# A row mean on one core: rows in parts of 16, 96 and 16, two stores behind the last load, and the last scaling on GpSimd

## The chip, the cores and the metric

One core of a Trainium2 chip. The metric is the device time of one execution in microseconds, median of several runs. "Span" is the profiled part of an execution, some 1.5 us shorter. Executions of one kernel mostly agree within 0.3%.

## The reference

```python
batch, seq, dim = 32, 512, 1024            # x: float32, 67.1 MB
def reference(x, divisor):                 # divisor = 1024.0
    return (np.sum(x, axis=-1) / divisor).astype(np.float32)
```

16384 rows of 4 KiB are read once, and one float is written for each.

## The kernel before

Each of the 128 partitions handles 128 rows: 112 of the main part and 16 of the last part, each contiguous in memory (the pitch from one partition to the next is 448 KiB in the main part and 64 KiB in the last). All loads are on one queue, into three bulk tiles in turn, then into small tiles of their own. VectorE (DVE) sums; ScalarE (ACT) takes some rows late in the kernel. The last two rows of a partition are cut to shorten the work after the last byte.

```python
    L = 16
    M = J - L                                    # 112
    x_main = bass.AP(tensor=x.tensor, offset=0, ap=[[M * D, P], [D, M], [1, D]])
    x_last = bass.AP(tensor=x.tensor, offset=P * M * D, ap=[[L * D, P], [D, L], [1, D]])
    # ... o_main and o_last alike
    main = [(2, 0)] + [(14, 0)] * 6 + [(14, 4), (12, 5)]      # (rows, of them on ACT)
    last = [(8, 4), (4, 2), (2, 1)]
    # ...
    res = one.tile([P, M], F32, name="res")
    fin = one.tile([P, L], F32, name="fin")
    q = one.tile([P, L], F32, name="q")
    r = one.tile([P, L], F32, name="r")
    nc.gpsimd.memset(r, 0.0)
    # ... loads and sums of main (into res) and of last (into q)
    c = 768
    row = one.tile([P, D], F32, name="row")
    load(row, x_last[:, j, :])
    act_sum(r[:, j : j + 1], row[:, c:], by=scale)
    nc.vector.reduce_sum(out=q[:, j : j + 1], in_=row[:, :c], axis=AX)

    a, b = 448, 704
    # ... pa, pb, pc: the last row's columns [:a], [a:b], [b:], each with its own load
    nc.gpsimd.tensor_scalar_mul(out=res, in0=res, scalar1=scale)
    tc.keep_in_program_order(nc.sync.dma_start(out=o_main, in_=res))

    act_sum(pc[:, D - b : D - b + 1], pa)
    nc.vector.reduce_sum(out=pc[:, D - b + 1 :], in_=pb, axis=AX)
    nc.vector.scalar_tensor_tensor(
        out=fin[:, : L - 1], in0=q[:, : L - 1], scalar=scale, in1=r[:, : L - 1], op0=MULT, op1=ADD
    )
    scaled = one.tile([P, D - b + 2], F32, name="scaled")
    nc.vector.tensor_scalar(
        out=scaled, in0=pc, scalar1=scale, scalar2=0.0, op0=MULT, op1=ADD, accum_out=fin[:, L - 1 :]
    )
    tc.keep_in_program_order(nc.sync.dma_start(out=o_last, in_=fin))
```

## Time and profile before

| | before |
|---|---|
| time, median of 4 runs | 161.5 us (161.36 to 161.53) |
| span of the profiled run | 159.8 us |
| DVE, ACT, GpSimd busy | 121.1, 19.6, 0.8 us |
| moved | 67.18 MB, 420 GB/s |
| end of the last DVE instruction | 158.28 us |

The prediction shows the lines and reads them. What to look for: the DMA rows are full from start to end, so the time is that of the bytes plus a tail; and in the tail DVE is the last to be ready. In the lines of the profile, L176 is line 176 of the kernel, SPq the queue that issues the DMAs, DVEq or ACTq the queue in front of that engine, and "issue" time in which the profile shows nothing waited for; the merged chain follows what ended last back through what released it. Below I also use the trace's landing records: each load signals from all sixteen DMA engines, and its landing is the last of the sixteen. They are not a printed view, so they stand in tables.

### The profile page before, as it was taken

Reading aid. Unit: us, or ns where it says so; the run is one execution under the profiler, and the core shown is the slowest. Engines: PE = TensorE matmul, PEld = TensorE weight load, DVE = VectorE, ACT = ScalarE, POOL = GpSimd, SP = SyncE. Lnnn points to the kernel's source line nnn. Section 1 sums busy time; section 2 is a strip of 40 time slices with the busy share of each in tenths; the row PEclk is TensorE's granted clock in tenths of the full one; section 3 lists DMA queues with packets and bytes.
Section 4 is the critical chain, followed back from the end, with each engine's and each line's share of the span. In section 5 each row is a group of like instructions: output and inputs, shape, how many; then the busy total and the mean of one; then the engine's idle time right before and its main releaser. Section 6 shows DMA issues by size and latency. Waiting matters only on the chain.

```text
span 159.8 us, 139 instructions
## 1 busy us (share of the span) xinstructions
DVE 121.1 (76%) x17; ACT 19.6 (12%) x37; POOL 0.8 (0%) x6
## 2 busy tenths in 40 slices
DVE  0500059995999599978999599959995996494985
ACT  3000000000000000000000000000001900480973
POOL 0000000000000000000000000000000000001000
DMA  7999999978999999978999999978999999899993
GB/s 250 472 459 459 459 459 459 459 330 359 459 459 459 459 459 459 459 316 373 459 459 459 459 459 459 416 345 388 459 459 427 394 480 505 353 435 390 408 400 132
DMA packets 2592, 67.18 MB, mean 420 GB/s; under 512 B 544, under 2 KB 928, under 8 KB 1056
## 3 DMA queue, kind: packets, MB, share of 16 engines
q1 hardware_dynamic: 2592, 67.18, 98.0%
HBM read 67.11 MB, written 0.07 MB: 420 GB/s over the span
## 4 chain that ended last, share of the span: by engine, by line
DMA 76%; DVE 22%; SPq 1%; issue 0%; DVEq 0%
DMA t<-in_x_dram 56%; DMA row<-in_x_dram 21%; DVE res L153 20%; SPq L142 1%; DVE q L176 1%; DVE scaled L198 0%; DVE pc L193 0%; DVE fin L194 0%; DVEq L198 0%; DVEq L232 0%
## 5 line engine op out<-in xcount | busy, mean ns | idle before, releaser
L153 DVE TENSOR_REDUCE res<-t 128x14 f32<-128x14336 f32 (+3 forms) x9 | 111.2, 12360 | 34.3 <-DMA t<-in_x_dram 34.3
L147 ACT ACTIVATE junk<-t 128x1024 f32<-128x1024 f32 x16 | 16.2, 1013 | 135.9 <-DMA t<-in_x_dram 135.9
L153 DVE TENSOR_REDUCE q<-t 128x4 f32<-128x4096 f32 (+2 forms) x3 | 7.9, 2642 | 2.7 <-DMA t<-in_x_dram 2.5
L147 ACT ACTIVATION_READ_ACCUMULATOR junk<-t 128x1 f32 x16 | 3.0, 187 | 0.0
L147 ACT ACT_TABLE_LOAD x1 | 1.3, 1283 | 1.7 <-PEq L218 1.7
L189 POOL TENSOR_SCALAR res<-res 128x112 f32<-128x112 f32 x1 | 0.5, 494 | 143.8 <-DVE res L153 143.8
L176 DVE TENSOR_REDUCE q<-row 128x1 f32<-128x768 f32 x1 | 1.0, 953 | 0.0
L198 DVE TENSOR_SCALAR_CACHE_REDUCE scaled<-pc 128x322 f32<-128x322 f32 x1 | 0.5, 490 | 0.1
L147 ACT ACTIVATE junk<-pa 128x448 f32<-128x448 f32 x1 | 0.5, 548 | 0.0
L193 DVE TENSOR_REDUCE pc<-pb 128x1 f32<-128x256 f32 x1 | 0.4, 414 | 0.0
L147 ACT ACTIVATE junk<-row 128x256 f32<-128x256 f32 x1 | 0.4, 388 | 0.1
L194 DVE SCALAR_TENSOR_TENSOR fin<-q,r 128x15 f32<-128x15 f32 x1 | 0.2, 176 | 0.0
L147 ACT ACTIVATION_READ_ACCUMULATOR junk<-pa 128x1 f32 x1 | 0.2, 186 | 0.0
L147 ACT ACTIVATION_READ_ACCUMULATOR junk<-row 128x1 f32 x1 | 0.2, 185 | 0.0
L139 POOL MEMSET r<- 128x16 f32 x1 | 0.1, 112 | 1.3 <-POOLq L218 1.3
L218 POOL MEMSET const-bfloat16-1.0<- 128x1 bf16 x1 | 0.1, 103 | 0.0
L218 POOL MEMSET const-uint8-127<- 128x1 uint8 x1 | 0.1, 102 | 0.0
L218 POOL MEMSET const-float32-0.0<- 128x1 f32 x1 | 0.1, 99 | 0.2 <-issue 0.2
L218 POOL MEMSET const-float32-1.0<- 128x1 f32 x1 | 0.1, 99 | 0.0
L198 DVE DVE_READ_ACCUMULATOR scaled<-pc 128x1 f32 x1 | 0.1, 83 | 0.0
## 6 DMA issues: line engine op xcount, KB each, us to landing
t<-in_x_dram SPq DMA_DIRECT2D x7, 7168.0 KB, 35.7
t<-in_x_dram SPq DMA_DIRECT2D x1, 6144.0 KB, 33.3
t<-in_x_dram SPq DMA_DIRECT2D x1, 4096.0 KB, 26.1
t<-in_x_dram SPq DMA_DIRECT2D x2, 1024.0 KB, 18.6
t<-in_x_dram SPq DMA_DIRECT2D x1, 2048.0 KB, 30.5
row<-in_x_dram SPq DMA_DIRECT2D x1, 512.0 KB, 33.2
pa<-in_x_dram SPq DMA_DIRECT2D x1, 224.0 KB, 33.3
pc<-in_x_dram SPq DMA_DIRECT2D x1, 160.0 KB, 33.1
```

What stands on the lines that cost most here:

```text
L139: nc.gpsimd.memset(r, 0.0)
L142: tc.keep_in_program_order(nc.sync.dma_start(out=dst, in_=src))
L147: nc.scalar.activation(junk[:, :n], src, COPY, scale=by, accum_out=dst)
L153: nc.vector.reduce_sum(out=dst[:, :d], in_=t[:, :d, :], axis=AX)
L176: nc.vector.reduce_sum(out=q[:, j : j + 1], in_=row[:, :c], axis=AX)
L189: nc.gpsimd.tensor_scalar_mul(out=res, in0=res, scalar1=scale)
L193: nc.vector.reduce_sum(out=pc[:, D - b + 1 :], in_=pb, axis=AX)
L194: nc.vector.scalar_tensor_tensor(out=fin[:, : L - 1], in0=q[:, : L - 1], scalar=scale, in1=r[:, : L - 1], op0=MULT, op1=ADD)
L198: nc.vector.tensor_scalar(out=scaled, in0=pc, scalar1=scale, scalar2=0.0, op0=MULT, op1=ADD, accum_out=fin[:, L - 1 :])
L218: nc = _bacc.Bacc("TRN2", target_bir_lowering=False, num_devices=1)
```

## The change

The intent: take the scaling of the first 15 results of the last part off DVE, which ends last, and give it to GpSimd; recut the last two rows to suit; scale the results of the main part in two tiles as they come, and store both behind the last load. The reads change with it: parts of 16, 96 and 16 rows per partition.

```diff
-    main = [(2, 0)] + [(14, 0)] * 6 + [(14, 4), (12, 5)]
+    parts = [[(2, 0), (14, 0)], [(14, 0)] * 5 + [(14, 4), (12, 5)]]
     last = [(8, 4), (4, 2), (2, 1)]
 ...
+    def rows_of(first, n):
+        return bass.AP(tensor=x.tensor, offset=first * P * D, ap=[[n * D, P], [D, n], [1, D]])
 ...
-    res = one.tile([P, M], F32, name="res")
+    res = [one.tile([P, n], F32, name=f"res{k}") for k, n in enumerate(sizes)]
-    r = one.tile([P, L], F32, name="r")
-    nc.gpsimd.memset(r, 0.0)
+    r = one.tile([P, 1], F32, name="r")
 ...
+        nc.gpsimd.tensor_scalar_mul(out=res[k], in0=res[k], scalar1=scale)     # after each part
 ...
-    c = 768
+    c = 688
-    act_sum(r[:, j : j + 1], row[:, c:], by=scale)
+    act_sum(r, row[:, c:], by=scale)
-    a, b = 448, 704
+    a, b = 480, 672
 ...
-    nc.gpsimd.tensor_scalar_mul(out=res, in0=res, scalar1=scale)
-    tc.keep_in_program_order(nc.sync.dma_start(out=o_main, in_=res))
+    for k, n in enumerate(sizes):
+        tc.keep_in_program_order(nc.sync.dma_start(out=means_of(sum(sizes[:k]), n), in_=res[k]))
 ...
-    nc.vector.scalar_tensor_tensor(
-        out=fin[:, : L - 1], in0=q[:, : L - 1], scalar=scale, in1=r[:, : L - 1], op0=MULT, op1=ADD
+    nc.gpsimd.tensor_scalar_mul(out=fin[:, :j], in0=q[:, :j], scalar1=scale)
+    nc.gpsimd.tensor_scalar(
+        out=fin[:, j : j + 1], in0=q[:, j : j + 1], scalar1=scale, scalar2=r, op0=MULT, op1=ADD
     )
```

More of the change, by code (lines that the diff above doesn't have):

```diff
@@ L117, with means_of @@
     assert J * P == N
-    L = 16
-    M = J - L
-    x_main = bass.AP(tensor=x.tensor, offset=0, ap=[[M * D, P], [D, M], [1, D]])
-    x_last = bass.AP(tensor=x.tensor, offset=P * M * D, ap=[[L * D, P], [D, L], [1, D]])
-    o_main = bass.AP(tensor=out.tensor, offset=0, ap=[[M, P], [1, M]])
-    o_last = bass.AP(tensor=out.tensor, offset=P * M, ap=[[L, P], [1, L]])
-    main = [(2, 0)] + [(14, 0)] * 6 + [(14, 4), (12, 5)]
-    last = [(8, 4), (4, 2), (2, 1)]
-    assert sum(n for n, _ in main) == M and sum(n for n, _ in last) == L - 2
+    parts = [[(2, 0), (14, 0)], [(14, 0)] * 5 + [(14, 4), (12, 5)]]
+    last = [(8, 4), (4, 2), (2, 1)]
+    L = sum(n for n, _ in last) + 2
+    sizes = [sum(n for n, _ in p) for p in parts]
+    assert sum(sizes) + L == J
+    def rows_of(first, n):
+        return bass.AP(tensor=x.tensor, offset=first * P * D, ap=[[n * D, P], [D, n], [1, D]])
+    def means_of(first, n):
+        return bass.AP(tensor=out.tensor, offset=first * P, ap=[[n, P], [1, n]])
+    x_last = rows_of(sum(sizes), L)
+    o_last = means_of(sum(sizes), L)
     bulk = ctx.enter_context(tc.tile_pool(name="bulk", bufs=3))
@@ L153, in sums @@
         nc.vector.reduce_sum(out=dst[:, :d], in_=t[:, :d, :], axis=AX)
-    j = 0
-    for rows, on_act in main:
-        t = bulk.tile([P, 14, D], F32, name="t")
-        load(t[:, :rows, :], x_main[:, j : j + rows, :])
-        sums(res[:, j : j + rows], t, rows, on_act)
-        j += rows
+    for k, part in enumerate(parts):
+        x_part = rows_of(sum(sizes[:k]), sizes[k])
+        j = 0
+        for rows, on_act in part:
+            t = bulk.tile([P, 14, D], F32, name="t")
+            load(t[:, :rows, :], x_part[:, j : j + rows, :])
+            sums(res[k][:, j : j + rows], t, rows, on_act)
+            j += rows
+        nc.gpsimd.tensor_scalar_mul(out=res[k], in0=res[k], scalar1=scale)
     j = 0
```

## The prediction

> **What bounds the kernel now.** I read the page's chain first, because it says what kind of thing the time is, then the rows in slices, then the merged chain, the timeline of the last microseconds and the waits of the queue that issues the DMAs.
>
> ```profile
> DMA 76%; DVE 22%; SPq 1%; issue 0%; DVEq 0%
> ...
> DMA  7999999978999999978999999978999999899993
> GB/s 250 472 459 459 459 459 459 459 330 359 459 459 459 459 459 459 459 316 373 459 459 459 459 459 459 416 345 388 459 459 427 394 480 505 353 435 390 408 400 132
> ```
>
> Bytes bound it. The DMA row is at 7 to 9 from the first slice to the last but one; 67.18 MB in 159.8 us is 420 GB/s. The 22% of DVE in the chain is misleading: two of the six long reductions (15.1 us each) are in it because a bulk load is issued only when a buffer comes free, but the DMA row stays full beside them. The landings say so more sharply: the loads of 14 rows land at 4.80, 21.74, 38.69, 55.62 and so on, 16.94 us apart each time (the trace's landing records), which is 7.34 MB / 16.94 us = 433 GB/s without a gap. (The dips to 316 to 373 are an artefact of booking long packets into slices: the landings show no gap there.) So in the body only bytes per microsecond count, and what is not bytes is the tail after the last loads.
>
> The tail in order of time, from the merged chain:
>
> ```profile
> 122.91 33.25 DMA row<-in_x_dram
> 156.16 0.02 issue
> 156.18 0.96 DVE q L176
> 157.14 0.03 issue
> 157.17 0.18 DVE fin L194
> 157.34 0.34 DVE pc L193
> 157.68 0.04 DVEq L198
> 157.72 0.07 issue
> 157.79 0.49 DVE scaled L198
> 158.28 0.01 DVEq L232
> ```
>
> From the landing of the last whole row (156.16) to the end of DVE (158.28) the chain is DVE's alone, 2.12 us. The other inputs of the last instruction, from the timeline of the tail and the issues with their time to landing:
>
> ```profile
> 156.72 0.55 ACT L147 ACTIVATE junk<-pa 128x448 f32<-128x448 f32 x1
> ...
> 157.20 0.19 ACT L147 ACTIVATION_READ_ACCUMULATOR junk<-pa 128x1 f32 x1
> ...
> 158.31 0.34 SPq L201 DMA_DIRECT2D out_dram<-fin  x1
> ```
>
> ```profile
> pa<-in_x_dram SPq DMA_DIRECT2D x1, 224.0 KB, 33.3
> pc<-in_x_dram SPq DMA_DIRECT2D x1, 160.0 KB, 33.1
> pb<-in_x_dram SPq DMA_DIRECT2D x1, 128.0 KB, 33.1
> out_dram<-res SPq DMA_DIRECT2D x1, 56.0 KB, 11.5
> out_dram<-fin SPq DMA_DIRECT2D x1, 8.0 KB, 1.4
> ```
>
> pa was issued at 123.39, pb at 123.87, pc at 124.39, the store of res at 146.17, so they landed at 156.7, 157.0, 157.5 and 157.7. ACT was done at 157.39. DVE itself, done with pb at 157.68, was the last thing that the final instruction waited for: 0.18 us later than the data.
>
> ```profile
> SPq L232 <- DMA out_dram<-res: 0.6, 1, 0.6
> ...
> SPq L201 <- DVE scaled L198: 0.5, 1, 0.5
> ```
>
> The store of fin also waits for the first store, since the drain in front of it waits for every other DMA. That came at 157.7; then 0.5 us were waited for DVE. So the first store has about 0.5 us of slack, no more.
>
> **What the Trainium skill says.** (1) "DMA: Bandwidth & Descriptors", section Queues, rings and completion order: each DMA engine takes descriptors of a ring in order. The trace agrees: the res store issued at 146.17 landed at 157.7, just behind pc (157.5), though its data was ready. (2) The same page, section Latency and other measured facts, warns of row pitches in HBM at large powers of two: copies at 512 KiB ran at 207 GB/s per direction against 214 for a padded pitch, at 2 MiB 164. The change alters the pitch, from 448 KiB (112 rows of 4 KiB) to 64 and 384 KiB. The trace of before has 64 KiB too, in its last part: the packets of 32768 bytes there took 1216 ns, 26.9 bytes per ns; a 14-row packet, 57344 bytes in 2.118 us, is 27.1. No difference. 384 KiB is not tried in it. (3) "SBUF — State Buffer", section Who interferes with whom: GpSimd shares ports with DVE, but a tensor_reduce on trn2 never contends, nor does the tensor_scalar form that writes an accumulator; a DVE instruction with two SBUF inputs does. All that DVE still does beside GpSimd in the new tail is of the harmless kinds. The trace of before doesn't show an overlap that could test it: its one GpSimd scaling (145.65) ran while DVE was idle. (4) "Perfetto Trace Analysis", GPSIMD Engine Instruction, calls the reported length of a GpSimd instruction unreliable; so I take GpSimd's 494 ns as rough.
>
> **The change, part by part.**
>
> *Body.* The same bytes in loads of the same sizes and in the same order; the order of instructions on DVE and ACT is the same save one removed on DVE. Pitch aside, nothing changes: 0 us. The memset of r at 1.73 us goes; it was beside the first load: 0. The scaling of the first 16 results moves to some 37 us, beside the loads: 0.
>
> *Stores of res.* One store of 128 packets of 448 bytes becomes two, of 64 and of 384 bytes. The first can be issued after the wait at about 138, the second after 147.6; both are still behind pc in every ring, issued by 124.8. Per engine 8 packets each: the records show 448-byte packets starting 21 ns apart, so 8 x 21 = 0.17 us; for 384 bytes about 18.5 ns and for 64 bytes about 8 ns (estimates from these and from fin's packets), 8 x 26.5 = 0.21 us, plus one semaphore packet of 9 ns. So they land at about 157.76 in place of 157.71. Slack of 0.5 us becomes some 0.25 (the next paragraph moves the other side). Not on the path, but near.
>
> *DVE in the tail.* The instruction of 176 ns (L194) goes: with its gaps it held the chain from 157.14 to 157.26, where pb's reduction began beside its end, so 0.12 us. The row's reduction goes from 768 to 688 columns: 768 took 953 ns, 256 took 414, so 1.05 ns a column, 80 x 1.05 = 0.08 us. Thus row 156.18 to 157.05. pb's reduction is of 192 in place of 256, 414 - 67 = 347 ns; it can start when pb is there, about 157.0, at 157.04 at most: done at 157.39. Before it was 157.68, so DVE is free 0.29 us earlier.
>
> *What the last instruction waits for then.* ACT: 336 columns of row in place of 256. ACT's 448 took 548 ns and 256 took 388, so 0.83 ns a column; the row takes 0.455 us, its read begins at 156.57. The next can start 0.09 later, as the others do (start to start 1.04 us, read begun after 0.97), 156.66; but pa, 32 columns larger, lands at about 156.74 (16 KB at 433 GB/s is 0.04 us). 156.76 + 0.575 = 157.33, the read of the accumulator to 157.45. And pc lands at 157.5 still: the bytes up to its end are the same. So of DVE 157.39, ACT 157.45, pc 157.50, pc is the last. With 0.02 to 0.1 us of start the last instruction begins at about 157.56, not 157.79. It has 354 columns, not 322: 32 x 1.05 = 0.03 us more, 0.52. Its end: 158.08, not 158.28. Saved on the path: 0.23 - 0.03 = 0.20 us.
>
> *GpSimd.* Its second instruction of the tail needs the row's sum (157.05). GpSimd started 0.09 us after DVE's end at 145.56; at the full 494 ns of the 112-column form it would be done at 157.05 + 0.09 + 0.49 = 157.63, with one column likely by 157.3. Before 158.08 in either case. The first (14 columns) needs 156.16, 0.9 us earlier. Beside: 0.
>
> *The end.* Store of fin: same 8 KB, 1.4 us from issue. Sum: 159.8 - 0.2 = 159.6 us of span, 161.5 - 0.2 = 161.3 us of time. I choose to subtract from the median of 161.5, although the runs lie between 161.36 and 161.5; the saving is of the size of that spread.
>
> **The rivals.** (a) *The stores take DVE's place.* If the two small stores land 0.4 us later than I say, at 158.2 or so, the drain in front of the last store is what ends last and the gain is nil, or a loss of up to 0.2: 161.4 to 161.7. For it: both stores are behind the last load, their packets are small, and the drain passes several semaphores after the late one. Against it: 8 packets per engine cost nanoseconds each in the trace of before, and fin's 64-byte packets are 11 ns long. (b) *GpSimd ends last.* Needs a tail instruction of over 0.9 us, or two of 0.9 us from 156.2; against it 494 ns for 112 columns. It would give 161.5 to 161.8. (c) *The pitch of 384 KiB slows the body.* 96 of 128 rows are read so; 1% of rate there would be 1.2 us (0.75 of 156), and 2.8% (3.2 us) a whole verdict. For it only the page's row for 512 KiB; against it that this row lost 3% only and that in this trace engines, not HBM, set a constant rate (16.94 us each time, and the same at 64 KiB). It would make 162 to 165. (d) *The gain is hidden.* If pc or ACT comes a little later than I have it, the saving is 0.1: 161.4.
>
> **Range and chances.** The middle is 161.3. (d) and the spread of the runs, 0.14 us in three, widen it by 0.2 upward and downward, (a) and (b) some more upward, and a different state of the chip some both ways: 160.9 to 161.7. A gain of 2% would be 3.2 us, more than the whole tail from 156.16: almost excluded, 0.01. A loss of 2% needs (c) at its worst or an oversight: 0.02. Within 2%: 0.97.
>
> **What would show it right or wrong.** Right: landings of the 14-row loads still 16.94 us apart; in the chain, no fin on DVE, the row's reduction about 0.87 us, the last DVE instruction starting at about 157.5 to 157.6 and 0.52 us long, waiting for pc or ACT rather than for DVE; the queue still waiting for DVE before the store of fin, issued at about 158.1; 2736 packets (128 more of data, 16 more of semaphores). Wrong by (a): the wait of the queue for out_dram as the last one, and the store issued later than DVE's end by over 0.1. By (b): GpSimd the last before the store. By (c): landings over 17 us apart in the middle part. What would make the number wrong with the steps right is a shift of all loads by a few tenths, which the first landing (4.80) would show.

## The result, and the profile after

161.87 us (161.55 to 162.17, 4 runs) against 161.5: ratio 1.0024, 95% interval 1.0004 to 1.0045. That is within 2%, but outside the predicted range and on the wrong side: 0.2 us less was expected, 0.37 us more came. The runs also spread more: 161.42 to 162.17 over the 14 runs that the changed kernel had in all.

The page of the changed kernel counts the packets forecast:

```profile
DMA packets 2736, 67.18 MB, mean 419 GB/s; under 512 B 688, under 2 KB 1072, under 8 KB 1200
```

The end of its merged chain:

```profile
123.65 33.83 DMA pa<-in_x_dram
157.47 0.02 issue
157.50 0.57 ACT junk L151
158.07 0.13 ACTq L240
158.20 0.03 issue
158.23 0.05 DVEq L206
158.28 0.08 issue
158.35 0.52 DVE scaled L206
158.88 0.01 DVEq L240
```

DVE's own work no longer sets the end. The chain now runs from the landing of pa through ACT to the last DVE instruction. And everything is later: pa landed at 157.47, not at the 156.7 of before. The timeline of the tail has DVE's and GpSimd's part of it, and the queue's waits the store:

```profile
156.79 0.87 DVE L183 TENSOR_REDUCE q<-row 128x1 f32<-128x688 f32 x1
...
157.76 0.35 DVE L200 TENSOR_REDUCE pc<-pb 128x1 f32<-128x192 f32 x1
157.76 0.27 POOL L202 TENSOR_SCALAR fin<-q,r 128x1 f32<-128x1 f32 x1 [0.71 <-DVE q L183]
...
158.91 0.33 SPq L209 DMA_DIRECT2D out_dram<-fin  x1
```

```profile
SPq L240 <- DMA out_dram<-res: 1.0, 1, 1.0
...
SPq L209 <- DVE scaled L206: 0.3, 1, 0.3
```

GpSimd (POOL) is done at 158.03, long before DVE. The queue still waits for DVE last, 0.3 us after the stores of res. So neither GpSimd nor the stores hold the end. Where the time went, by the landing records and the lines above (us):

| stretch | before | after | difference | predicted difference |
|---|---|---|---|---|
| start to the first landing | 4.80 | 4.86 | +0.06 | 0 |
| first landing to that of the 12-row load | 133.12 | 133.52 | +0.40 | 0 |
| 12-row load to 8-row load | 9.71 | 9.70 | -0.01 | 0 |
| 8-row load to row | 8.53 | 8.69 | +0.16 | 0 |
| row's landing to the end of DVE | 2.12 | 2.11 | -0.01 | -0.20 |
| end of DVE to the end of the span | 1.48 | 1.47 | -0.01 | 0 |

The differences add up to 0.59 us, that of the spans (159.76 and 160.35). Three things are to be explained: 0.40 us lost in the body, 0.16 us lost in the last loads, and a tail that gained nothing. The body can also be seen in a printed view, the stretch from 20 to 125 us (columns: length, busy time and instructions of DVE, ACT and GpSimd, clock, DMA share, GB/s), first before, then after:

```profile
20.00:125.00 105.00, 92.11 (x7) 1.59 (x3) 0.00 (x0) 1.00 1.00 434
```

```profile
20.00:125.00 105.00, 91.70 (x7) 1.18 (x3) 0.26 (x1) 1.00 1.00 430
```

The DMA engines are full in both and move 434 and 430 GB/s. So packets themselves last longer. The packet records agree: of the 896 packets of the 14-row loads none was over 20 ns longer than their median (2116 ns) before; after, 119 were, by up to 210 ns, and all of them in the part with 96 rows. I call such packets slow. The sign that the prediction set for rival (c), landings over 17 us apart in the middle part, is there in the last two 14-row loads (17.07 and 17.15 us).

### The profile page after: what moved, and what is told of

Same layout as the page of the kernel before. It is cut to its first block, busy times and chain, and to the rows that moved or that the text cites. A ratio compares the mean times of both kernels' runs of the same rounds, so it can differ in the third digit from the quotient of the medians.

```text
span 160.4 us, 143 instructions
## 1 busy us (share of the span) xinstructions
DVE 120.9 (75%) x16; ACT 19.7 (12%) x37; POOL 1.4 (1%) x8
## 4 chain that ended last, share of the span: by engine, by line
DMA 77%; DVE 21%; SPq 1%; ACT 0%; issue 0%; ACTq 0%; DVEq 0%
DMA t<-in_x_dram 56%; DMA pa<-in_x_dram 21%; DVE res L157 20%; SPq L146 1%; ACT junk L151 0%; DVE scaled L206 0%; ACTq L240 0%; DVEq L206 0%; DVEq L240 0%
## 5 line engine op out<-in xcount | busy, mean ns | idle before, releaser
L167 POOL TENSOR_SCALAR res<-res 128x16 f32<-128x16 f32 (+1 forms) x2 | 0.7, 354 | 145.4 <-DVE res L157 145.4
L183 DVE TENSOR_REDUCE q<-row 128x1 f32<-128x688 f32 x1 | 0.9, 870 | 0.1
L206 DVE TENSOR_SCALAR_CACHE_REDUCE scaled<-pc 128x354 f32<-128x354 f32 x1 | 0.5, 523 | 0.2 <-ACT junk L151 0.2
L151 ACT ACTIVATE junk<-pa 128x480 f32<-128x480 f32 x1 | 0.6, 574 | 0.1
L151 ACT ACTIVATE junk<-row 128x336 f32<-128x336 f32 x1 | 0.5, 455 | 0.1
```

Of the source, the lines that this page charges most:

```text
L151: nc.scalar.activation(junk[:, :n], src, COPY, scale=by, accum_out=dst)
L167: nc.gpsimd.tensor_scalar_mul(out=res[k], in0=res[k], scalar1=scale)
L206: nc.vector.tensor_scalar(out=scaled, in0=pc, scalar1=scale, scalar2=0.0, op0=MULT, op1=ADD, accum_out=fin[:, L - 1 :])
```

## The experiments

There were eighteen runs on four chips: fifteen new kernels, the changed kernel twice more and one version a second time. Each was compared with the kernel before on the same chip, 5 rounds; its times there lay between 161.23 and 161.49 on all of them.

### Taking the change apart

**again**: the changed kernel, unaltered.

> The changed kernel once more, unaltered, to see whether its loss and its spread repeat. Theory P (the row pitch of 384 KiB in the middle part slows some packets of the loads): about 161.85 us again, with a spread of some 0.5 us between runs, and in the trace some 100 or more of the 896 packets of the 14-row loads over 20 ns longer than their median, all after 21 us, where the 96-row part begins. Theory R (a disturbance by chance of the one trace): slow packets elsewhere or none, and the time back at 161.5 or under.

161.66 us against 161.29, ratio 1.0023 (1.0011 to 1.0036). 102 slow packets, two of them ahead of the 96-row part; body 133.59 us, 8-row load to row 8.69. The loss repeats.

**layout_only**: only the addresses.

```diff
-        load(t[:, :rows, :], x_main[:, j : j + rows, :])
+        first, n = (0, 16) if j < 16 else (16, M - 16)
+        x_part = bass.AP(tensor=x.tensor, offset=first * P * D, ap=[[n * D, P], [D, n], [1, D]])
+        load(t[:, :rows, :], x_part[:, j - first : j - first + rows, :])
 ...  # and the one store of res as two, 16 and 96 columns
```

> The kernel before with only the addresses changed: rows in parts of 16, 96 and 16, hence two stores; same tiles in SBUF, same work on DVE, ACT and GpSimd. Theory P: as slow as the changed kernel or slower, 161.8 to 162.2, slow packets in the middle part, landings late by some 0.4 us at 123 us. Theory S (the new places of the tiles in SBUF, or GpSimd's scaling at 38 us, slow the loads): no slow packets, 161.5. Theory T (the loss lies in the tail): 161.5.

161.68 us, less than Theory P's 161.8 to 162.2, ratio 1.0023 (1.001 to 1.0035), 59 slow packets. The addresses alone can make as much as the whole loss, and no tile had moved. Its profiled run doesn't show the late body forecast, though (133.16 us): there the time was lost at the load of row, 33 of whose packets were slow.

**stores_only**: the store of res as two at the old pitch.

```diff
-    tc.keep_in_program_order(nc.sync.dma_start(out=o_main, in_=res))
+    for k, n in ((0, 16), (16, 96)):
+        o_part = bass.AP(tensor=out.tensor, offset=k, ap=[[M, P], [1, n]])
+        tc.keep_in_program_order(nc.sync.dma_start(out=o_part, in_=res[:, k : k + n]))
```

> The kernel before with its one store of res made in two, of 16 and of 96 columns, at the old row pitch of 448 KiB. Prices the extra store alone. Theory P: 161.5 within 0.1, since the store lands at most 0.1 us later and the last store still waits for DVE; no slow packets. Theory W (the extra store holds up the end): 161.7 or more, with the queue's last wait for out_dram rather than for DVE.

161.37 us, ratio 1.0004 (0.999 to 1.0018), no slow packets. The extra store is as good as free, as predicted.

**tail_only**: the changed kernel with its first two parts joined, so the old pitch and one store, but the new tail.

```diff
-    parts = [[(2, 0), (14, 0)], [(14, 0)] * 5 + [(14, 4), (12, 5)]]
+    parts = [[(2, 0)] + [(14, 0)] * 6 + [(14, 4), (12, 5)]]
```

> The changed kernel with its first two parts joined: row pitch of 448 KiB and one store as before, but the new tail (GpSimd scaling, the new cuts 688, 480 and 672). Theory P: the predicted gain comes out in part, 161.3 to 161.45, no slow packets; the last DVE instruction waits for ACT, since it started 0.15 us after ACT's end in the changed kernel, not 0.06. Theory T (the loss lies in the new tail): 161.8 as the changed kernel.

161.54 us, ratio 1.0015 (1.0003 to 1.0028), no slow packets. Both theories missed in the time: no gain, but not the whole loss either. (The last DVE instruction did wait for ACT, as Theory P has it.) The body is that of before (133.11 us), the last loads are not: 8-row load to row 8.69 us, as in the changed kernel, not 8.53. The chain shows what that does:

```profile
123.48 33.62 DMA pa<-in_x_dram
...
157.12 0.57 ACT junk L151
...
157.98 0.52 DVE scaled L206
```

pa landed at 157.10, 0.4 us later than before, and the end hangs on pa now. What of the new tail could make earlier loads slower, of 4 and 2 rows, that it doesn't touch? Only their place. The compiled programs give the start of each tile within a partition. Before, the tail's tiles start at 189184 bytes, a multiple of 64 (and of 256); with the shorter r at 189152, 32 lower.

### The place of the tail's tiles

**shift_only**: the kernel before with r longer by 8 columns that nothing uses.

```diff
-    r = one.tile([P, L], F32, name="r")
+    r = one.tile([P, L + 8], F32, name="r")[:, :L]
```

> The kernel before with the tile r longer by 8 columns, which nothing uses: every tile of the tail then lies 32 bytes further in each partition, off the multiples of 64 that they had. The changed kernel shortens r to one column and so shifts them by 32 too. Theory A (the shift slows the writes of the last loads): from the landing of the 8-row load to that of pc some 10.05 us, as in the changed kernel and in tail_only, not the 9.87 of before; 161.45 where before is 161.3. Theory C (the cuts at columns 480 and 672, off the multiples of 64 columns, do it): 9.87 and no loss.

161.5 us against 161.36, ratio 1.0005 (0.9992 to 1.0019), so the time alone is unclear. The landings are not: 10.08 us from the 8-row load to pc, as Theory A said, where before had 9.87. The plainest part of it is in the 4- and 2-row loads: the second landed 7.41 us behind the 8-row load, not 7.27. (The load of row varies from run to run whatever the place, so from here on these two loads tell more than the sum to pc.)

**tail_aligned**: tail_only with r back at 16 columns.

```diff
-    r = one.tile([P, 1], F32, name="r")
+    r = one.tile([P, 16], F32, name="r")[:, :1]
```

> The new tail at the old row pitch, as tail_only, but with r of 16 columns again of which one is used, so the tail's tiles lie on multiples of 64 bytes as before. Theory A: 9.87 to 9.93 us from the 8-row load to pc and a gain at last: 161.2 where before is 161.3. Theory C: as tail_only, 10.08 us and plus 0.2.

161.31 us against 161.36, ratio 0.9993 (0.9981 to 1.0006). That is 0.0022 under tail_only (0.35 us), with nothing changed but 60 unused bytes. The 4-row and 2-row loads came 7.25 us behind the 8-row load, where tail_only had 7.39; to pc it took 9.96 us, a little over the forecast. pa landed at 156.87. The gain over the kernel before, forecast at 0.1 us, is not clear of noise. The same pieces of its chain as shown for tail_only:

```profile
156.90 0.57 ACT junk L151
...
157.75 0.52 DVE scaled L206
```

Both are 0.22 to 0.23 us earlier than in tail_only.

**after_aligned**: the changed kernel with the same edit.

```diff
-    r = one.tile([P, 1], F32, name="r")
+    r = one.tile([P, 16], F32, name="r")[:, :1]
```

> The changed kernel with r of 16 columns, one used, so that the tail's tiles lie on multiples of 64 bytes again. Theory A (the shift by 32 bytes costs 0.2 us in the tail, the pitch the rest): from the 8-row load to pc 9.85 to 9.95 us, not 10.08; the time 161.4 to 161.55 where before is 161.35 and the changed kernel was 161.66 beside 161.29. If the shift has no effect beside the pitch: 161.7.

161.4 us against 161.38, ratio 0.9997 (0.9984 to 1.0011): the changed kernel with this one edit equals the kernel before. The time fell a little below the forecast. The landings met it in the 4- and 2-row loads (7.28 us), not in the sum to pc (10.15), since row itself was late in the profiled run, the slowest of the five (1.52 us behind the 2-row load, 1.26 before).

**shift_64** asks whether multiples of 64 are what counts:

```diff
-    r = one.tile([P, L], F32, name="r")
+    r = one.tile([P, L + 16], F32, name="r")[:, :L]
```

> As shift_only but r longer by 16 columns, so that the tail's tiles move by 64 bytes and stay on multiples of 64. Theory A (off the multiples of 64 bytes, the writes of the loads cost some 3 to 5 ns more per packet): as before, packets of 16384 bytes at 611 ns and not 614, from the 8-row load to pc 9.87 us, the time within 0.05 us of before. Theory A2 (any other place of the tiles costs, for example by the side of SBUF they reach): as shift_only, 10.08 us.

161.45 us against 161.3, ratio 1.0008 (0.9995 to 1.0021); 10.07 us. A shift by 64 costs what one by 32 does: Theory A in its first form is wrong.

**shift_bulk** moves the bulk tiles by 32 bytes (and the tail's tiles, by the sum of both edits, by 64):

```diff
+    pads = ctx.enter_context(tc.tile_pool(name="pads", bufs=1))
+    pad = pads.tile([P, 8], F32, name="pad")
+    nc.gpsimd.memset(pad, 0.0)
     bulk = ctx.enter_context(tc.tile_pool(name="bulk", bufs=3))
 ...
-    r = one.tile([P, L], F32, name="r")
+    r = one.tile([P, L + 8], F32, name="r")[:, :L]
```

> The kernel before with a tile of 32 bytes ahead of the three bulk tiles, and r longer by 8 columns, so that only the bulk tiles lie off the multiples of 64 bytes and the tail's tiles on them. Theory A with a cost per packet of 4 ns: 10 bulk loads of 8 packets per engine, 0.3 us later at the 8-row load, 161.65 where before is 161.35. Theory A with a cost per byte (3 ns in 16384 bytes): 10 ns for each 57344-byte packet, 0.8 us in all, 162.2. Theory A3 (the shift matters only for the short loads): 161.35.

161.46 us, ratio 1.0007 (0.9994 to 1.0021). The body took 133.16 us: moving the bulk tiles by 32 costs nothing, so both sizes forecast for it fell. The tail took 10.06, as for any shift by 64. The bulk tiles of before start 128 past a multiple of 256, the tail's on one. Hence the next form: multiples of 256.

**bulk_256**: a pad of 128 bytes ahead of the bulk tiles, r unaltered. Bulk tiles start on multiples of 256, the tail's 128 past one.

```diff
+    pads = ctx.enter_context(tc.tile_pool(name="pads", bufs=1))
+    pad = pads.tile([P, 32], F32, name="pad")
+    nc.gpsimd.memset(pad, 0.0)
     bulk = ctx.enter_context(tc.tile_pool(name="bulk", bufs=3))
```

> The kernel before with an unused tile of 128 bytes ahead of the bulk tiles. It moves the bulk tiles from 128 past a multiple of 256 bytes onto a multiple, and the tail's tiles from a multiple to 128 past one. Theory A256 (what counts is multiples of 256 bytes, and each packet off them costs some 8 to 12 ns): the eight loads from the first landing to that of the 12-row load take 132.4 us, not 133.1 (64 packets per engine by 10 ns is 0.6 to 0.7), and from the 8-row load to pc 10.05, not 9.87; the time some 0.5 us under before, 160.8. Theory A128 (multiples of 128 do): 133.1 and 9.87, no change of time. Theory A3 (the place counts only for the short loads): 133.1 and 10.05, plus 0.15 us.

161.31 us against 161.32, ratio 1.0002 (0.999 to 1.0015). Body 132.93 us, tail 10.04. The direction is that of Theory A256 in both, the size not: (133.12 - 132.93) us over 64 packets per engine is 3 ns a packet (an estimate from the landings), not 8 to 12. What the body won the tail lost.

**all_256** is told with the versions at the end.

### The pitch

**layout_30_82**: layout_only with parts of 30 and 82 rows (pitches 120 and 328 KiB).

```diff
-        first, n = (0, 16) if j < 16 else (16, M - 16)
+        first, n = (0, 30) if j < 30 else (30, M - 30)
 ...  # and the two stores of 30 and 82 columns
```

> The kernel before, with rows in three parts and two stores like the layout run, but of 30, 82 and 16 rows, so that the main pitches are 120 and 328 KiB (15 and 41 times 8 KiB) in place of 64 and 384 KiB (3 times 128 KiB). Theory P2 (it is the large power of two in 384 KiB that slows packets): no slow packets among the 14-row loads, time as stores_only, within 0.1 us of before. Theory P1 (any split of the rows, or any pitch other than the old one, costs): some 60 to 120 slow packets and plus 0.3 us, as with 384 KiB.

161.61 us against 161.36, ratio 1.0017 (1.0005 to 1.003); no slow packet. For the time it was a bad experiment. Its stores have 120 and 328 bytes per partition, and these are what ends last:

```profile
SPq L236 <- DMA out_dram<-res: 1.7, 1, 1.7
```

```profile
157.91 0.49 DVE L202 TENSOR_SCALAR_CACHE_REDUCE scaled<-pc 128x322 f32<-128x322 f32 x1
...
158.76 0.33 SPq L205 DMA_DIRECT2D out_dram<-fin  x1
```

The second store landed at 158.57, 0.95 us behind pc, and the last store went out 0.36 us after DVE's end at 158.40; in the kernel before it goes out 0.03 us after. This is rival (a) of the prediction, met elsewhere. Stores of 64 and 384 bytes landed 0.34 us behind pc (stores_only).

**reads_30_82** and **reads_16_96** leave the store as it was and so put results in wrong places; only the reads differ from before.

```diff
-        load(t[:, :rows, :], x_main[:, j : j + rows, :])
+        first, n = (0, 30) if j < 30 else (30, M - 30)        # or 16 in place of 30
+        x_part = bass.AP(tensor=x.tensor, offset=first * P * D, ap=[[n * D, P], [D, n], [1, D]])
+        load(t[:, :rows, :], x_part[:, j - first : j - first + rows, :])
```

> Wrong on purpose in the same way, with parts of 30 and 82 rows, pitches of 120 and 328 KiB. Its correct brother was held up by its stores of 120 and 328 bytes per partition, which landed 0.95 us behind pc, so its time told nothing of the pitch. Theory P2: no slow packets and within 0.1 us of before. Theory P1 (any split costs): plus 0.3 us.

> Wrong on purpose: the kernel before with only the places that its loads read from changed to parts of 16 and 96 rows; the store stays one and puts sums in the wrong places. It leaves no store in doubt. Theory P2 (pitch of 384 KiB slows packets): 50 to 120 slow packets among the 14-row loads, 161.6 to 161.8 where before is 161.35. Theory W2 (half of the layout's loss was its second store): 161.4 to 161.5.

reads_30_82: 161.52 us against 161.38, a little more than Theory P2's 0.1 us, ratio 1.0011 (0.9999 to 1.0024), 2 slow packets, both in the first 5 us; body 133.11 as before. Its first load landed at 5.05, not 4.80, and the delay stayed to the end. reads_16_96: 161.6 us against 161.38, ratio 1.0012 (1.000 to 1.0025), 69 slow packets, body 133.30, runs from 161.23 to 161.75. So the slow packets come with 384 KiB, not with any split. In time the two splits can't be told apart.

**pitch_512**: one part of 128 rows.

```diff
-    x_main = bass.AP(tensor=x.tensor, offset=0, ap=[[M * D, P], [D, M], [1, D]])
-    x_last = bass.AP(tensor=x.tensor, offset=P * M * D, ap=[[L * D, P], [D, L], [1, D]])
+    x_main = bass.AP(tensor=x.tensor, offset=0, ap=[[J * D, P], [D, M], [1, D]])
+    x_last = bass.AP(tensor=x.tensor, offset=M * D, ap=[[J * D, P], [D, L], [1, D]])
 ...  # o_main and o_last alike
```

> The kernel before with all 128 rows of a partition in one piece, pitch 512 KiB throughout, one store as before; the same tiles. Theory P2: slow packets all through the body, more than the 60 to 120 of 384 KiB, and 161.8 to 165. Theory P1: 161.3, since nothing is split.

161.81 us against 161.36, ratio 1.0027 (1.0015 to 1.004); 40 slow packets, one by 731 ns; body 133.45. Fewer slow packets than the forecast, but the time is in its range. Counted over all runs:

| pitch of most loads | profiled runs | slow 14-row packets (of 896) |
|---|---|---|
| 448 KiB | 11 | 0 in nine, 1, 3 |
| 328 KiB | 2 | 0, 2 |
| 384 KiB | 6 | 119, 102, 69, 59, 29, 9 |
| 512 KiB | 1 | 40 |

### A version that beats both

**tail_cuts**: tail_aligned with the last row cut as before.

```diff
-    a, b = 480, 672
+    a, b = 448, 704
```

> A version meant to beat both: old pitch, tail on multiples of 64 bytes, scaling on GpSimd and the row cut at 688, but the last row cut at 448 and 704 as before. In all runs with the new cuts the last DVE instruction began 0.15 to 0.16 us after ACT's end, so ACT was what it waited for; here ACT has 32 columns less, and the last instruction too. By the working: ACT done 1.23 us after the row's landing, DVE 1.31, pc 1.34, the last instruction from 1.42 to 1.91 after it, where before it ended 2.12 after it. 161.15 to 161.25 where before is 161.35. Rival: the data's landing sets it and it equals the run with the new cuts, 0.05 under before.

161.12 us against 161.38, ratio 0.9986 (0.9973 to 0.9998). The end of its chain:

```profile
156.15 0.87 DVE q L183
157.02 0.43 DVE pc L200
157.44 0.03 DVEq L206
157.48 0.07 issue
157.55 0.49 DVE scaled L206
158.04 0.01 DVEq L240
```

Row landed at 156.12, so the last instruction runs from 1.43 to 1.92 us after it; 1.42 to 1.91 had been worked out, against 2.12 before. This is the gain that the change was made for: DVE goes from row's reduction, 80 columns shorter, straight to pb's.

**tail_cuts2** and **again2**: this version and the changed kernel once more, on one chip.

> The best version once more, unaltered, beside the changed kernel on the same chip: 161.1 to 161.2 where before is 161.3 to 161.4, ratio about 0.9986 to 0.999.

> The changed kernel a third time, beside the best version on the same chip: 161.65 to 161.85, ratio about 1.0023, some 60 to 120 slow packets in the middle part. From the first landing to that of pc about 153.3 us (152.7 before): 0.2 of it by the shift, the rest by the pitch. If the pitch costs nothing and only the shift does, 152.9.

161.12 us, ratio 0.9987 (0.9974 to 0.9999), and 161.53, ratio 1.0017 (1.0004 to 1.0029), against 161.3. The changed kernel's profiled run (161.42) had only 9 slow packets and a body of 133.15; another run took 162.03. From the first landing to pc it took 153.03 us, nearer to the 152.9 of the shift alone than to the 153.3 forecast. So the pitch's loss varies from run to run, and the shift's does not: the 4- and 2-row loads took 7.39 us.

**all_256**: tail_cuts with the pad of 128 bytes and r of 48 columns, so that all tiles of loads start on multiples of 256 (pb and pc too).

```diff
+    pad = pads.tile([P, 32], F32, name="pad")
 ...
-    r = one.tile([P, 16], F32, name="r")[:, :1]
+    r = one.tile([P, 48], F32, name="r")[:, :1]
```

> The best version (tail_cuts) with every tile that a load writes on a multiple of 256 bytes, bulk and tail. Theory A256: 132.4 and 9.78 us, 160.4 to 160.5 where before is 161.35, ratio about 0.9945. Theories A128 and A3: as the best version, 161.12.

161.03 us against 161.32, ratio 0.9982 (0.9969 to 0.9996). The lowest time of all, but not clear of tail_cuts, and far from the 160.4 forecast. The body took 132.95 us, as in bulk_256, while the 4- and 2-row loads took 7.36, more than the 7.25 to 7.33 of the eleven profiled runs with the tail at its old place. So "on a multiple of 256 or not" doesn't describe the tail either.

## Why the prediction was wrong

**Right: the reading of the bound, and the prices of instructions.** Bytes bound the kernel, and this change could gain in the tail alone. (One line is misread, without consequence: the landing at 4.80 is that of the 2-row load; the 14-row loads land from 21.74 on, at the spacing given.) Row's reduction took 870 ns as worked out, ACT's two 455 and 574 (455 and 575), pb's 353 (347), the last DVE instruction 523 (520). GpSimd needed 267 ns and did not hold the end, so rival (b) was rightly set aside, and the stores (rival a) too. It ran beside DVE's reductions, which took their predicted times, so they show no contention. Taking work off DVE is worth what was predicted: in tail_cuts DVE ends 1.92 us after row's landing, 2.12 before, of which the removed instruction is 0.12 and the 80 columns 0.08. That the changed kernel too was predicted to end DVE at 1.92 (158.08 - 156.16) is in part luck: that figure had other cuts, and pc last instead of DVE.

**Wrong: "And pc lands at 157.5 still: the bytes up to its end are the same."** The bytes are the same, their place in SBUF isn't. Shortening r moved the tail's tiles by 32 bytes; the prediction treated r's new size as the loss of a memset only. In shift_only, with all else as before, a move by 32 bytes put pc at 157.73. The landings show it in every run: in the nine profiled runs with the tail's tiles elsewhere than at 189184 the 4- and 2-row loads took 7.36 to 7.41 us, in the eleven with them there 7.25 to 7.33.

In time, the shift costs 0.0005 to 0.0008 in the old tail (shift_only, shift_64, shift_bulk, each unclear by itself). In the new tail undoing it gave 0.0022 (tail_only to tail_aligned) and 0.0020 to 0.0027 (the changed kernel's 1.0017, 1.0023 and 1.0024 to after_aligned's 0.9997), some 0.35 us. Two such ratios, taken on different chips, have a difference that is uncertain by some 0.0018 either way. So that there is an effect is just clear of the noise; its size is not, and the two traces of tail_only and tail_aligned account for 0.23 us of the 0.35. That it weighs more in the new tail fits with (but is not shown by) the end hanging on pa, which is behind three shifted loads and its own: pa landed 0.70 us after row in the changed kernel and 0.59 in tail_aligned; 0.58 was predicted. By the times this is the larger part of the changed kernel's loss on average, and undoing it alone brings the changed kernel level with the kernel before. In the one profiled run of the result the body lost more (0.40 us, below).

**Mis-sized: "With 0.02 to 0.1 us of start".** The last instruction was taken to wait for pc, which starts an instruction 0.02 us after landing, as other loads show. It waited for ACT, and from ACT's end to its start went 0.15 us in the changed kernel (158.20 to 158.35) and as much in tail_aligned. (This is argued: in four of the six profiled runs with the new cuts the profile names pc, which landed up to 0.03 us behind ACT's end. But from ACT's end to the start it is 0.15 or 0.16 us in all six, from pc's landing 0.12 to 0.20.) With the new cuts ACT has 32 columns more of the last row and 80 more of the one before, which leaves it last. This is rival (d) of the prediction, and with the shift undone its size is right: in tail_aligned DVE ends 2.00 us after row's landing, so 0.12 us of the 0.20 are left. tail_cuts gives the 32 columns back and has 1.92.

**Wrong in size: "Pitch aside, nothing changes: 0 us", and rival (c), priced at 162 to 165.** The pitch of 384 KiB does slow packets: all six profiled runs with it have 9 to 119, runs with other pitches under 512 KiB at most 3. The body took 133.30 to 133.59 us in three of the six profiled runs with it and 133.13 to 133.16 in the others, within the 133.09 to 133.16 of the runs at 448 KiB with bulk tiles in the old place or 32 bytes on. (Two of those others, layout_only and after_aligned, lost time at row instead: it landed 1.60 and 1.52 us behind the 2-row load, in all other runs 1.22 to 1.36.) In time the pitch is the less certain part, and in the new tail the smaller one: 0.0012 (reads_16_96) to 0.0019 (layout_only less stores_only), but only 0.0002 to 0.0009 between kernels with the new tail that differ in the layout (the changed kernel and tail_only; after_aligned and tail_aligned). With some 0.0018 of noise either way these agree; they don't add up neatly with the shift, and I don't settle the share.

**What stays open.** Why the place of the tail's tiles counts: they were slower at -32, +32, +64 and +128 bytes from 189184, and in part still at +256 together with moved bulk tiles. A rule of multiples fits the body and not all of the tail. Nor does it show in the packets' own lengths throughout: those of 16384 bytes took 615.5 ns on average in tail_only, but 611.0 in the changed kernel, where before has 611.3. Why 384 and 512 KiB slow packets is not shown either, nor why the first load of some layouts lands 0.2 us late, nor what slows a varying number of row's packets (33 of 128 in layout_only, 16 before; 0, 0 and 14 in the three traces of the changed kernel).

## What to carry to other kernels

In a kernel bound by its loads, any edit that resizes a small tile or re-addresses a load can move the addresses of the others: compare the start of every loaded tile and the landings of loads you did not touch before you explain a small loss by the instructions you changed. Take a change apart: here one line (r) and one layout hid a real gain of 0.14%, which the version without them has. When you move work off the engine that ends last, work out what is last then, and price its handover from a measured handover between those two engines.

## What the Trainium skill lacked or had wrong

- "SBUF — State Buffer", Operand start alignment, says of itself that it is about legality and not speed and that its runs timed nothing. The place of a load's destination has a price: with the tail's tiles moved by 32 to 128 bytes the 4- and 2-row loads took 7.38 to 7.41 us behind the 8-row load, 7.25 to 7.33 at their old place; bulk tiles moved by 128 bytes onto multiples of 256 took 132.93 us, not 133.1 (3 ns a packet). "DMA: Bandwidth & Descriptors", How a descriptor splits into AXI transactions, has descriptors that start off 256-byte boundaries cost more beats, told of the bytes that are fetched; here it is the written side that moved. The body agrees in direction, the tail (all_256, 7.36 us for two loads against 7.25 to 7.33) not throughout.
- "DMA: Bandwidth & Descriptors", Latency and other measured facts, gives the effect of the row pitch for copies between HBM tensors at powers of two from 512 KiB. For loads into SBUF it is there at 384 KiB too, and small: 9 to 119 of 896 packets slowed by 20 to 230 ns; at 512 KiB the time rose by 0.27%.
- "GPSIMD Engine Reference", Engine selection, calls one-input elementwise work roughly line-rate. Here 14 and 16 columns took 263 and 258 ns and 112 took 494: some 2.5 ns a column ((494 - 258) / 96), where DVE's tensor_scalar takes 1.03 ((523 - 490) / 32), and by the same estimate some 220 ns before the first. ("Perfetto Trace Analysis", GPSIMD Engine Instruction, rightly warns that such reported lengths are unreliable.)
- No page gives the delay from the end of an engine's instruction, or of a load, to the start of the instruction that waits for it: ACT's last accumulator read to DVE 0.15 us, a DVE instruction to the next that waits for it 0.11, a landed load to its reader 0.02.
- No page tells for this chip how late small stores behind the last load land, by their size per partition: 120 and 328 bytes landed 0.95 us behind the last load, 64 and 384 bytes 0.34, one store of 448 bytes 0.21.
